# Input projections in groups of two or three column tiles, with 128 of the 576 tokens as the stationary operand

## The chip, the cores and the metric

The kernel runs on one core of one Trainium2 chip. The metric is device time in microseconds of one execution. The engines are named as the profile names them: PE is TensorE (PEld its weight loads), DVE is VectorE, ACT is ScalarE, POOL is GpSimd, SP is SyncE, which issues all DMAs here.

## The reference

One step of a hybrid encoder layer, for a prompt of 512 tokens and a sample of 64 tokens, 2048 channels:

```
mod = silu(c) @ w_ada + b_ada;  shift, scale, gate = split(mod)
h = rmsnorm(x) * (1 + scale) + shift
q|k|v|z_att|u_ssm|z_ssm|u_pool|z_pool = h @ w_in      # 2048 x 6144
y_att  = chunk-band attention (16 heads of 64, relative bias)
y_ssm  = complex-diagonal state-space scan of u_ssm -> gelu -> GLU
y_pool = trailing means (2/4/8/16) of u_pool minus token, linear, scale
y = concat(rmsnorm_b(y_b) * silu(z_b))
x = x + gate * (y @ w_out);  final rmsnorm
```

It returns the layer's output, the keys and values, and the states. All is float32. The kernel keeps float32 accuracy in its large products by splitting each operand into a rounded part and a rest (h into `hh` and `hl`, a weight into `wh` and `wl`) and adding three passes: hh by wh, hl by wh, hh by wl.

## The kernel before, in words

All 576 tokens (512 prompt, 64 sample) go together. Activations lie with channels on partitions and tokens along the free dimension, in tiles of four blocks of 128 channels (`ck`, 14 buffers). The 6144 columns of w_in are 48 column tiles of 128.

- First block (to about 139 us): adaLN, norm and modulation, one 128-channel block at a time, and with it six of the column tiles (`first_tiles`: Q, K of head pairs 0 and 1, V of pairs 0 and 2). Its order is written out by hand. Their results for the prompt lie in six PSUM banks, four of them of pool `pp` (`fA`, `fB`).
- Attention stage (139 to about 490 us): the other 22 tiles of V, K, Q and u, one column tile at a time by `proj_steps` (L486), interleaved with the attention of eight head pairs (`att_units`). `evac_q`, `evac_k` and `evac_v` empty a projection's PSUM.
- Gate and pool stage (490 to about 697 us): 16 tiles (z of attention, u and z of pooling) interleaved with the state-space branch (`s5_units`), evacuated by `gate_z` and `pool_branch`.
- GLU, then the last four z tiles (751 to 803 us), then the output product and final norm.

`proj_steps` computes one column tile in 16 steps, one for each block of 128 channels. A step issues six matmuls: three passes, each for two halves of 288 tokens, with the weight block stationary and the tokens moving. The result takes a tile of two PSUM banks from `pp`, which has two such tiles, so that one is filled while the other is emptied. The other four banks are pool `pm` (`mtile`), used by attention, the scan and all small products.

Weights come in chunks of 128x1024 (eight channel blocks of one column tile). `w_next` loads and splits ahead: a chunk is loaded by SP, cast by ACT into `wh` (L146), and DVE subtracts to get `wl` (L70, a helper for all subtractions), up to two chunks ahead of the one in use; each of the three kinds of buffer has three copies.

`evac_q` empties a Q tile for two heads: for each head, ACT writes the rounded part to one half of the partitions, then DVE writes the rest to the other half:

```
A.activation(Q1[a, c0:c0 + n], ps[a], AF.Copy, scale=0.125)
stt(Q1[o, c0:c0 + n], ps[a], 0.125, Q1[a, c0:c0 + n].bitcast(F32), ALU.mult, ALU.subtract)
```

`gate_z` applies Silu on ACT into a single buffer `z` and then multiplies on DVE.

`interleave(gens, units, total)` sets the order in which the code writes projection steps and units: one unit after so many steps. Outside the blocks with a hand-written order, a planner then sets the order on each engine: it simulates the program with its own durations and takes, of the instructions that are ready, the one written first. So an engine's order needn't be the code's. At run time each engine follows its fixed order and waits where it must. The planner also keeps two engines from one PSUM bank at a time, by waits.

Of the kernel before, what the change touches and what calls it, by code (L numbers as in the profile page):

```python
# [17 lines left out]
NP = 512  # L18
# [3 lines left out]
HC = NT // 2  # L22
NH = 16
# [8 lines left out]
S5_SPREAD = 231  # L32
# [16 lines left out]
def kernel(ctx, tc, xp, xs, xT, cT, wada_ss, wada_g, bsh, bsc, bgate, ng, wf1, wrest,  # L49
# [68 lines left out]
    pp = psctx.enter_context(tc.tile_pool(name="pp", bufs=2, space=PSUM))  # L118
# [4 lines left out]


    wsrc = [wrest[r, :, 8 * h:8 * h + 8] for r in range(38) for h in range(2)]
    wsrc += [wglu[f] for f in range(4)]
    wsrc += [wrest[r, :, 8 * h:8 * h + 8] for r in range(38, 42) for h in range(2)]
# [4 lines left out]
    def w_load():  # L132
        n = wstate[0]
        t = wp.tile([128, 1024], F32, tag="wr", name="w", bufs=WR)
        src = wsrc[n]
        SY.dma_start(t.rearrange("p (a b) -> p a b", a=src.shape[1]), src)
        wraw[n] = t
        wstate[0] += 1

    def w_split():  # L140
        n = wstate[1]
        while wstate[0] <= n:
            w_load()
        t = wraw.pop(n)
        wh = wp.tile([128, 1024], F32R, tag="wh", name="wh")
        A.copy(wh, t)  # L146
        wl = wp.tile([128, 1024], F32R, tag="wl", name="wl")
        sub(wl, t, wh.bitcast(F32))
        wsplit[n] = (wh, wl)
        wstate[1] += 1  # L150
# [215 lines left out]
    warm = pp.tile([128, 2, 512], F32, tag="pj", name="warm")  # L366
    for n in range(WARM):
        PE.matmul(warm[:, 0, 0:128], ident, xc[3][:, WLANE, 0:128], start=True, stop=True)
# [19 lines left out]
    rb = pp.tile([128, 2, 512], F32, tag="pj", name="rb")  # L388
    rstdx = s1.tile([128, NT], F32, tag="rstdx", name="rstdx", bufs=1)
    for t in range(5):  # L390
        V.tensor_scalar(dg[:, t], ident, r[:, t:t + 1], None, op0=ALU.mult)
        if t < 4:
            PE.matmul(rb[:, 0, 128 * t:128 * t + 128], ones, dg[:, t], start=True, stop=True)
        else:
            PE.matmul(rb[:, 1, 0:64], ones, dg[:, t, 64:128], start=True, stop=True)
    split_w(0)
    ada_sel(0)
    A.copy(rstdx[:, NP:NT], rb[:, 1, 0:64])
    A.copy(rstdx[:, 0:NP], rb[:, 0])

    fA = pp.tile([128, 2, 512], F32, tag="pj", name="fA")
    fB = pp.tile([128, 2, 512], F32, tag="pj", name="fB")
    fC = mtile("fC")
    fD = mtile("fD")
    fS = mtile("fS", (128, 384))
    f1p = [fA[:, 0], fA[:, 1], fB[:, 0], fB[:, 1], fC, fD]
# [79 lines left out]
    def f1_pieces(f):  # L486
        return [(f1p[f], 0, NP), (fT[:, 64 * f:64 * f + 64], NP, NS)]
# [3 lines left out]
    def proj_steps(done):  # L491

        ps = pp.tile([128, 2, 512], F32, tag="pj", name="pj")
        for k in range(KT):
            if k % 8 == 0:
                wh, wl = w_next(8)
            c, i = divmod(k, 4)
            for ws, hs, first, last in ((wh, hh, True, False), (wh, hl, False, False), (wl, hh, False, True)):
                for ch in range(2):
                    PE.matmul(ps[:, ch, 0:HC], ws[:, k % 8], hs[c][:, i, HC * ch:HC * ch + HC],  # L500
                              start=(k == 0 and first), stop=(k == KT - 1 and last))
            if k == KT - 1:
                nxt = done(ps)
                if callable(nxt):
                    pend.append(nxt)
            yield
            if k in (2, 7, 12) and pend:
                nxt = pend.pop(0)()
                if callable(nxt):
                    pend.append(nxt)  # L510

    def pj_pieces(ps):
        return [(ps[:, 0, 0:HC], 0, HC), (ps[:, 1, 0:NP - HC], HC, NP - HC), (ps[:, 1, NP - HC:HC], NP, NS)]

# [17 lines left out]
    kvs, Q1s, Tbs = {}, {}, {}  # L532
# [9 lines left out]
    def kv_load(j):  # L542
        kv = ck("kv", F32, (128, 2304))
        kf, vf = kv[:, 0:704], kv[:, 704:704 + NT]
        vt = kv[:, 1280:2048].rearrange("p (b d) -> p b d", b=6)
        SY.dma_start(kf[:, NP:NP + 128], ckT[j])
        SY.dma_start(vt[:, 4], cv[:, j])
        G.memset(vt[64:128, 5], 0.0)
        kvs[j] = (kf, vf, vt)

# [4 lines left out]
    def evac_q(j, pieces):  # L555
        Q1 = ap1.tile([128, 2 * NT], F32R, tag="Q1", name="Q1", bufs=2)
        Q1s[j] = Q1
        for ps, t0, n in pieces:
            for h in range(2):
                a, o = halves[h]  # L560
                c0 = q_col(h, t0)
                A.activation(Q1[a, c0:c0 + n], ps[a], AF.Copy, scale=0.125)
                stt(Q1[o, c0:c0 + n], ps[a], 0.125, Q1[a, c0:c0 + n].bitcast(F32), ALU.mult, ALU.subtract)

    def evac_k(j, pieces):
        kf = kvs[j][0]
        for ps, t0, n in pieces:
            o = t0 if t0 < NP else 640
            A.copy(kf[:, o:o + n], ps)
        SY.dma_start(k_o[j, :, 0:NP], kf[:, 0:NP])  # L570
        SY.dma_start(k_o[j, :, NP:NT], kf[:, 640:704])

    def evac_v(j, pieces):
        if j not in kvs:
            kv_load(j)
        vf = kvs[j][1]
        for ps, t0, n in pieces:
            V.tensor_copy(vf[:, t0:t0 + n], ps)

    def att_units(j):  # L580
# [15 lines left out]
        def vtr():  # L596
            pv = mtile("pv", (128, 4, 128))
            for i in range(4):
                PE.transpose(pv[:, i], vf[:, 128 * i:128 * i + 128], ident)
            pw = mtile("pw", (128, 128))  # L600
            PE.transpose(pw[0:64], vf[:, NP:NT], ident)
            A.copy(vt[:, 0:4], pv)
            A.copy(vt[0:64, 5], pw[0:64])
# [90 lines left out]
    kv_load(2)  # L694
    first.close()
    evac_v(0, f1_pieces(2))
    evac_k(0, f1_pieces(1))
    evac_q(0, f1_pieces(0))
    evac_q(1, f1_pieces(3))
    evac_k(1, f1_pieces(4))  # L700
    evac_v(2, f1_pieces(5))

    def proj_v(j):
        yield from proj_steps(lambda ps: evac_v(j, pj_pieces(ps)))

    def proj_kq(j):
        att_load(j)
        for e in (evac_k, evac_q):
            yield from proj_steps(lambda ps, e=e: e(j, pj_pieces(ps)))

    def proj_u(f):
        yield from proj_steps(lambda ps: evac_u(f, ps))
# [3 lines left out]
    def evac_u(f, ps):  # L716
        if f == 0:
            uTs.append(ck("uT"))
        A.copy(uTs[0][:, f].rearrange("p (c t) -> p c t", c=2), ps[:, :, 0:HC])

    interleave([proj_v(1), proj_kq(2), proj_v(3)], att_units(0) + att_units(1), 64)
    for j in range(2, 7):
        units = att_units(j)
        interleave([proj_kq(j + 1), proj_v(j + 2) if j < 6 else proj_u(0)], units, 48)
    interleave([proj_u(f) for f in range(1, 4)], att_units(7), 48)
# [6 lines left out]
    ysp0 = yp_.tile([128, 8, 128], F32R, name="ysp0")  # L732
# [163 lines left out]
    def gate_z(y, ps):  # L896
        z = zp.tile([128, 2, HC], F32, tag="z", name="z")
        with tc.high_priority():
            A.activation(z, ps[:, :, 0:HC], AF.Silu)
        yv = y.rearrange("p (c t) -> p c t", c=2)  # L900
        mul(yv, yv, z)
# [7 lines left out]
    def gate_att(f, ps):  # L909
        y = y_att[f // 4][:, f % 4]  # L910
        stt(y, y, prm[:, 3, f:f + 1], ssqa, ALU.mult, ALU.mult)
        gate_z(y, ps)
# [8 lines left out]
    ypool = []  # L921

    def pool_branch(g, ps):
        wn = 2 << g
# [7 lines left out]
        for pv_, t0, n in pj_pieces(ps):  # L932
            o = 15 + t0 if t0 < NP else 542
            A.copy(e[:, o:o + n], pv_)
# [43 lines left out]
    gens = [proj_steps(lambda ps, f=f: gate_att(f, ps)) for f in range(8)]  # L978
    gens += [proj_steps(lambda ps, g=g: pool_branch(g, ps)) for g in range(4)]
    gens += [proj_steps(lambda ps, f=f: gate_z(ypool[0][:, f], ps)) for f in range(4)]  # L980
# [22 lines left out]
    for f in range(4):  # L1003
        wh, wl = w_next(4)
        ps2 = {}
        for part in (1, 0):
            if part == 0:
                pg_ = pp.tile([128, 2, 512], F32, tag="pj", name="pg")
                ps = [pg_[:, chn, 0:HC] for chn in range(2)]
# [11 lines left out]
        stt(y_ssm[:, f].rearrange("p (c t) -> p c t", c=2), pg_[:, :, 0:HC], bg[:, f:f + 1], sg, ALU.add, ALU.mult)  # L1021
# [24 lines left out]
    interleave([proj_steps(lambda ps, f=f: gate_z(y_ssm[:, f], ps)) for f in range(4)], [ssm_scale], 4)  # L1046
# [8 lines left out]
    ysp1 = fin.tile([128, 8, 128], F32R, name="ysp1", bufs=1)  # L1055
    ysp = [(ysp0, ysp1)[k // 8][:, k % 8] for k in range(KT)]
# [208 lines left out]
def _layout(i):  # L1265
# [64 lines left out]
_INS = ["xp", "xs", "xT", "cT", "wada_ss", "wada_g", "bsh", "bsc", "bgate", "ng", "wf1", "wrest", "ext", "ckT", "cv",  # L1330
# [40 lines left out]
```

## Time and profile before

| | |
|---|---|
| median of 3 runs | 1023.0 us (1022.98 to 1025.25) |
| profiled execution | 1021.69 us, span 1019.9 us |
| PE busy | 995.2 us, 7032 matmuls |
| DVE busy | 708.4 us |
| ACT busy | 456.8 us |

The span runs from the first to the last instruction; the profiled execution's own time is 1.8 us longer. Busy time is a union of an engine's instructions. A matmul's duration is a latency that overlaps its neighbours, so what it costs is read from the distance between starts.

### The profile page before, as it was taken

To read this page: it belongs to the slowest core of one execution; us is meant where nothing else is said; L and a number is where in the kernel's file an instruction comes from. 1 tells how busy PE (TensorE), PEld (TensorE's weight loads), DVE (VectorE), ACT (ScalarE), POOL (GpSimd) and SP (SyncE) were. 2 spreads that over 40 slices of the span, in tenths; PEclk is the share of its full clock that TensorE was granted. 3 is DMA by queue.
4 is the path that set the end of the run, shared out by engine and by line. 5 is a ranking of instruction groups with operands and counts; after the bars stand their busy time and mean duration, and the time that the engine had idled before them with its cause. 6 is when DMAs were issued, how large, how long until landed. Compare 5 with 4: busy or idle time off the path is not lost.

```text
span 1019.9 us, 17854 instructions
## 1 busy us (share of the span) xinstructions
PE 995.2 (98%) x7032; PEld 904.5 (89%) x7032; DVE 708.4 (69%) x1654; ACT 456.8 (45%) x873; POOL 7.1 (1%) x52
## 2 busy tenths in 40 slices
PE   4999999999999999999999999999999999999996
PEld 3666689999999999999999999999999988888885
DVE  5677785745555564644699897995353699988876
ACT  5332365635354453543835554658452414131325
POOL 0000000000000000000000000000000000000000
PEclk9999999999999999999999999999999999999998
DMA  9999652332333333222222212222322685646425
GB/s 365 412 417 388 239 174 78 100 103 89 88 95 98 100 96 100 75 74 83 66 79 77 84 63 86 78 66 67 100 84 83 234 297 181 226 142 207 140 92 196
DMA packets 51572, 148.45 MB, mean 146 GB/s; under 512 B 9312, under 2 KB 18528, under 8 KB 46816
## 3 DMA queue, kind: packets, MB, share of 16 engines
q1 hardware_dynamic: 51488, 147.31, 42.7%
q8 instruction: 55, 0.90, 0.4%
q14 instruction: 29, 0.24, 0.1%
HBM read 137.75 MB, written 9.53 MB: 144 GB/s over the span
## 4 chain that ended last, share of the span: by engine, by line
PE 96%; DMA 1%; DVE 1%; ACT 1%; SPq 0%; issue 0%; DVEq 0%
PE pj L500 52%; PE po L1128 6%; PE po L1127 6%; PE po L1129 6%; PE pa L330 3%; PE sps L629 2%; PE tp L645 2%; PE av L656 2%; PE po L1132 1%; PE po L1131 1%; PE pg L1016 1%; PE pgb L1016 1%; PE fS L442 1%; PE fA L436 1%; DMA xc<-in_xT_dram 1%; PE yp L885 1%
## 5 line engine op out<-in xcount | busy, mean ns | idle before, releaser
L500 PE MATMUL pj<-hh,wh 128*128 128x288 f32 x1344 | 298.0, 303 | 0.0
L500 PE MATMUL pj<-hh,wl 128*128 128x288 f32 x1344 | 287.8, 296 | 0.0
L500 PE MATMUL pj<-hl,wh 128*128 128x288 f32 x1344 | 287.7, 296 | 0.0
L500 PEld LDWEIGHTS pj<-hh,wh 128*128 128x128 f32 x1344 | 214.8, 189 | 3.4 <-issue 0.8
L500 PEld LDWEIGHTS pj<-hh,wl 128*128 128x128 f32 x1344 | 216.2, 188 | 0.1
L500 PEld LDWEIGHTS pj<-hl,wh 128*128 128x128 f32 x1344 | 215.6, 188 | 0.1
L146 ACT CAST wh<-w 128x1024 fp32r<-128x1024 f32 x120 | 125.8, 1049 | 176.5 <-PE po L1131 97.6
L70 DVE TENSOR_TENSOR wl<-w,wh 128x1024 fp32r<-128x1024 f32 x120 | 146.6, 1222 | 82.3 <-ACT wh L146 81.2
L1128 PE MATMUL po<-wl,yh 128*128 128x512 f32 (+1 forms) x256 | 99.0, 387 | 0.0
L1127 PE MATMUL po<-wh,yh 128*128 128x512 f32 (+1 forms) x256 | 99.0, 387 | 0.0
L1129 PE MATMUL po<-wh,yl 128*128 128x512 f32 (+1 forms) x256 | 99.0, 387 | 0.0
L76 DVE SCALAR_TENSOR_TENSOR acc<-ada,scT,acc 128x512 f32<-128x512 f32 x120 | 83.0, 747 | 0.5
L631 DVE CUSTOM_DVE_ANT_0 P<-sps,Tb 128x128 f32<-128x128 f32 (+2 forms) x80 | 36.9, 462 | 47.5 <-PE sps L629 41.3
L634 ACT ACTIVATE P<-P,s 128x128 f32<-128x128 f32 (+4 forms) x72 | 39.7, 551 | 66.2 <-DVE s L633 65.8
L1127 PEld LDWEIGHTS po<-wh,yh 128*128 128x128 f32 x256 | 48.1, 188 | 9.9
L1128 PEld LDWEIGHTS po<-wl,yh 128*128 128x128 f32 x256 | 48.1, 188 | 9.8
L1129 PEld LDWEIGHTS po<-wh,yl 128*128 128x128 f32 x256 | 48.1, 188 | 9.8
L629 PE MATMUL sps<-K,Q 128*128 128x128 f32 (+4 forms) x160 | 35.0, 307 | 0.1
L635 DVE RECIPROCAL s<-s 128x1 f32<-128x1 f32 x72 | 11.7, 163 | 33.4 <-ACT P L634 32.9
L650 ACT COPY PT<-tp 128x256 f32<-128x256 f32 (+1 forms) x40 | 18.3, 458 | 31.7 <-PE tp L645 31.5
L645 PE MATMUL tp<-ident,P 128*128 128x128 f32 x176 | 31.1, 273 | 0.0
L67 DVE TENSOR_TENSOR ssqa<-ssqa,sq 128x576 f32<-128x576 f32 x7 | 5.3, 761 | 37.1 <-ACT sq L672 37.1
(330 smaller groups left out, 1381.7 us busy)
## 6 DMA issues: line engine op xcount, KB each, us to landing
w<-in_wrest_dram SPq DMA_DIRECT2D x84, 512.0 KB, 3.7
ada<-in_wada_ss_dram SPq DMA_DIRECT2D x22, 1024.0 KB, 9.0
w<-in_wout_dram SPq DMA_DIRECT2D x32, 512.0 KB, 3.7
ada<-in_wada_g_dram SPq DMA_DIRECT2D x32, 512.0 KB, 4.5
adac<-in_wada_ss_dram SPq DMA_DIRECT2D x10, 1024.0 KB, 14.0
w<-in_wf_dram SPq DMA_DIRECT2D x16, 384.0 KB, 11.2
xc<-in_xT_dram SPq DMA_DIRECT2D x8, 576.0 KB, 7.4
Tb<-in_ext_dram SPq DMA_DIRECT2D x8, 512.0 KB, 3.7
```

The costliest lines, as they stand in the source:

```text
L70: V.tensor_tensor(o, a, b, op=ALU.subtract)
L76: V.scalar_tensor_tensor(o, in0=a, scalar=s, in1=b, op0=op0, op1=op1)
L146: A.copy(wh, t)
L330: PE.matmul(pa[32 * g:32 * g + 32, 0:256], sc[:, k], adat[b, k // 8][:, k % 8], start=(k < 4), stop=(k >= KT - 4))
L500: PE.matmul(ps[:, ch, 0:HC], ws[:, k % 8], hs[c][:, i, HC * ch:HC * ch + HC], start=(k == 0 and first), stop=(k == KT - 1 and last))
L629: PE.matmul(ps[:, n], qs, K[z][:, g, k0:k0 + nk], start=(z == 0), stop=(z == 1))
L631: V.tensor_tensor_reduce(out=p[r, 0:nk], in0=ps[r, n], in1=Tb[r, g, ::-1][:, b0:b0 + nk], scale=1.0, scalar=-3.0e38, op0=ALU.add, op1=ALU. ...
L634: A.activation(p[:, 0:nk], p[:, 0:nk], AF.Exp, bias=s4[:, 1:2], accum_out=s4[:, 2:3])
L645: PE.transpose(tp[:, kb], p[:, 128 * kb:128 * kb + 128], ident)
L1127: PE.matmul(po[t], yh[c][:, ci, s_], wh[:, i], start=f0, stop=False)
L1128: PE.matmul(po[t], yh[c][:, ci, s_], wl[:, i], start=False, stop=False)
L1129: PE.matmul(po[t], yl[c][:, ci, s_], wh[:, i], start=False, stop=l0)
```

## The change

Projections are computed in groups. Ten groups have three column tiles (K, Q, V of a head pair for pairs 2 to 7; two tiles of z_att with one of u_pool, four times), six have two (u_ssm, z_pool, z_ssm). For the first 448 tokens (NA) the weights stay stationary and one matmul of 448 columns takes the place of a half. For the last 128 tokens (NB: 64 of the prompt and the sample's 64) the tokens are stationary and the group's weights move, 384 or 256 columns at once. That result has tokens on partitions; it is copied to SBUF and transposed back by PE, tile by tile (`bt`), except V, which attention wants that way.

Pool `pp` becomes four tiles of one bank. A group of three takes all four. Weight chunks hold two channel blocks of three tiles (128x768) or four of two tiles (128x1024). In the last chunk of a group the 128 tokens come first, then the tiles one after another. The first block computes K, V, Q of pairs 0 and 1. The interleaving counts are adapted (ATT_SPREAD, S5_SPREAD), the sample's split buffers `ysp0` and `ysp1` hold 4 and 12 tiles instead of 8 and 8, and the GLU takes two one-bank tiles.

```diff
+NA = 448
+NB = NT - NA
-    pp = psctx.enter_context(tc.tile_pool(name="pp", bufs=2, space=PSUM))
+    pp = psctx.enter_context(tc.tile_pool(name="pp", bufs=4, space=PSUM))
...
-    def proj_steps(done):
-        ps = pp.tile([128, 2, 512], F32, tag="pj", name="pj")
-        for k in range(KT):
-            if k % 8 == 0:
-                wh, wl = w_next(8)
-            c, i = divmod(k, 4)
-            for ws, hs, first, last in ((wh, hh, True, False), (wh, hl, False, False), (wl, hh, False, True)):
-                for ch in range(2):
-                    PE.matmul(ps[:, ch, 0:HC], ws[:, k % 8], hs[c][:, i, HC * ch:HC * ch + HC],
-                              start=(k == 0 and first), stop=(k == KT - 1 and last))
...
+    def proj_group(done, done_b, bs):
+        nf = len(done)
+        kc = 2 if nf == 3 else 4
+        n = 0
+        for ch in range(KT // kc):
+            last = ch == KT // kc - 1
+            wh, wl = w_next(kc)
+            if ch == 0:
+                pa = [pjtile("pj") for _ in range(nf)]
+                pb = pjtile("pjb")
+            parts = list(range(nf)) + [nf]
+            if last:
+                parts = parts[-1:] + parts[:-1]
+            for f in parts:
+                for kk in range(kc):
+                    k = kc * ch + kk
+                    c, i = divmod(k, 4)
+                    f0, l0 = k == 0, k == KT - 1
+                    if f < nf:
+                        wsl = slice(128 * f, 128 * f + 128)
+                        PE.matmul(pa[f][:, 0:NA], wh[:, kk, wsl], hh[c][:, i, 0:NA], start=f0, stop=False)
+                        PE.matmul(pa[f][:, 0:NA], wh[:, kk, wsl], hl[c][:, i, 0:NA], start=False, stop=False)
+                        PE.matmul(pa[f][:, 0:NA], wl[:, kk, wsl], hh[c][:, i, 0:NA], start=False, stop=l0)
+                    else:
+                        o = pb[:, 0:128 * nf]
+                        PE.matmul(o, hh[c][:, i, NA:NT], wh[:, kk], start=f0, stop=False)
+                        PE.matmul(o, hh[c][:, i, NA:NT], wl[:, kk], start=False, stop=False)
+                        PE.matmul(o, hl[c][:, i, NA:NT], wh[:, kk], start=False, stop=l0)
+                    if l0 and f == nf:
+                        b_ = bs()
+                        nt = b_.shape[1] // 128
+                        with tc.high_priority():
+                            A.copy(b_, pb[:, 0:128 * nt])
+                    if l0 and f < nf:
+                        nxt = done[f](pa[f][:, 0:NA])
+                        if callable(nxt):
+                            pend.append(nxt)
+                    if l0 and f == nf - 2:
+                        bt = mtile("bt", (128, nt, 128))
+                        for g in range(nt):
+                            PE.transpose(bt[:, g], b_[:, 128 * g:128 * g + 128], ident)
+                        done_b(bt, pb)
+                    yield
...
+    def group_kqv(j):
+        def b(bt, pb):
+            vt = kvs[j][2]
+            V.tensor_copy(vt[64:128, 3], pb[0:64, 256:384])
+            V.tensor_copy(vt[0:64, 5], pb[64:128, 256:384])
+            evac_k(j, [(bt[:, 0], NA, NB)])
+            store_k(j)
+            evac_q(j, [(bt[:, 1], NA, NB)])
+        return proj_group([lambda ps, e=e: e(j, [(ps, 0, NA)]) for e in (evac_k, evac_q, evac_v)], b,
+                          lambda: (kv_load(j), kvt[j][:, 2048:2304])[1])
...
+    def z_a(y, ps):
+        z = zp.tile([128, NA], F32, tag="z", name="z")
+        with tc.high_priority():
+            A.activation(z, ps, AF.Silu)
+        mul(y[:, 0:NA], y[:, 0:NA], z)
```

## Rows read from the trace of the kernel before

**Rows 1.** The page, busy us of each engine, share of the span, instructions.
```profile
PE 995.2 (98%) x7032; PEld 904.5 (89%) x7032; DVE 708.4 (69%) x1654; ACT 456.8 (45%) x873; POOL 7.1 (1%) x52
```

**Rows 2.** The page, chain that ended last: shares of the span.
```profile
PE 96%; DMA 1%; DVE 1%; ACT 1%; SPq 0%; issue 0%; DVEq 0%
```

**Rows 3.** Waits: who waited for whom: us in total, times, longest.
```profile
PE warm L368 <- DMA xc<-in_xT_dram: 14.0, 1, 14.0
...
ACT Q L562 <- DVE Q L76: 9.6, 13, 0.9
```

**Rows 4.** The page, costliest groups: busy us, mean ns, idle before.
```profile
L500 PE MATMUL pj<-hh,wh 128*128 128x288 f32 x1344 | 298.0, 303 | 0.0
```

**Rows 5.** The chain in order of time: start us, us, what.
```profile
507.54 0.87 PE xtp L791 x8
...
699.07 26.38 PE pj L500 x198
...
755.76 47.60 PE pj L500 x357
```

**Rows 6.** Timeline of PE, output stage: start us, us, engine, line, operation.
```profile
809.80 0.39 PE L1128 MATMUL po<-wl,yh 128*128 128x512 f32 x1
...
815.92 0.39 PE L1127 MATMUL po<-wh,yh 128*128 128x512 f32 x1
...
1006.32 0.28 PE L1127 MATMUL po<-wh,yh 128*128 128x256 f32 x1
...
1008.00 0.28 PE L1129 MATMUL po<-wh,yl 128*128 128x256 f32 x1
```

**Rows 7.** Windows: length, busy of PE, PEld, DVE, ACT, POOL, clock, DMA, GB/s.
```profile
139.00:490.00 351.00, 350.85 (x2689) 337.29 (x2689) 199.26 (x554) 169.45 (x367) 4.62 (x37) 1.00 0.30 94
490.00:697.00 207.00, 207.00 (x1596) 204.20 (x1595) 183.10 (x434) 116.90 (x229) 0.33 (x3) 1.00 0.26 78
```

**Rows 8.** Timeline of ACT and DVE in the attention stage, Q's evacuation.
```profile
237.89 0.78 ACT L592 CAST K<-kv 64x704 fp32r<-64x704 f32 x1
...
239.42 0.39 ACT L562 ACTIVATE Q<-pj 64x288 fp32r<-64x288 f32 x1
...
240.31 0.45 DVE L76 SCALAR_TENSOR_TENSOR Q<-pj,Q 64x288 fp32r<-64x288 f32 x1
...
242.45 0.46 DVE L76 SCALAR_TENSOR_TENSOR Q<-pj,Q 64x288 fp32r<-64x288 f32 x1
...
247.88 0.23 DVE L76 SCALAR_TENSOR_TENSOR Q<-pj,Q 64x64 fp32r<-64x64 f32 x1
```

**Rows 9.** Timeline, end of the first block: Q of pair 0 evacuated.
```profile
135.50 0.59 ACT L562 ACTIVATE Q<-fA 64x512 fp32r<-64x512 f32 x1
...
137.56 0.69 DVE L76 SCALAR_TENSOR_TENSOR Q<-fA,Q 64x512 fp32r<-64x512 f32 x1
```

**Rows 10.** Timeline of ACT and DVE, gate and pool stage, Silu and product.
```profile
517.11 0.64 ACT L899 ACTIVATE z<-pj 128x576 f32<-128x576 f32 x1
...
525.66 0.75 DVE L64 TENSOR_TENSOR yatt<-yatt,z 128x576 f32<-128x576 f32 x1
...
567.00 1.28 ACT L899 ACT_TABLE_LOAD   x1
568.30 0.65 ACT L899 ACTIVATE z<-pj 128x576 f32<-128x576 f32 x1
...
570.96 0.75 DVE L64 TENSOR_TENSOR yatt<-yatt,z 128x576 f32<-128x576 f32 x1
```

**Rows 11.** Groups by line: weight splits of 1024 and 768 columns, ACT, DVE.
```profile
L146 ACT CAST wh<-w 128x1024 fp32r<-128x1024 f32 x120 | 125.8, 1049 | 176.5 <-PE po L1131 97.6 <-PE pj L500 54.9 <-PE pg L1016 8.5
...
L382 ACT CAST w1h<-w 128x768 fp32r<-128x768 f32 x16 | 13.1, 821 | 4.2 <-DMA w<-in_wf_dram 4.2
...
L70 DVE TENSOR_TENSOR wl<-w,wh 128x1024 fp32r<-128x1024 f32 x120 | 146.6, 1222 | 82.3 <-ACT wh L146 81.2 <-DMA ER<-in_scr_dram 0.6
...
L70 DVE TENSOR_TENSOR w1l<-w,w1h 128x768 fp32r<-128x768 f32 x16 | 15.3, 954 | 4.1 <-ACT w1h L382 4.1
```

More of the change, by code (lines that the diff above doesn't have):

```diff
@@ L122, in mtile, with pjtile, group_chunks @@
         return pm.tile(list(shape), F32, tag="m", name=name)
-    wsrc = [wrest[r, :, 8 * h:8 * h + 8] for r in range(38) for h in range(2)]
+    def pjtile(name, shape=(128, 512)):
+        return pp.tile(list(shape), F32, tag="pj", name=name)
+    def group_chunks(groups, g3, g2):
+        out = []
+        for g in groups:
+            if len(g) == 3:
+                out += [wg3[g3, :, 2 * n:2 * n + 2] for n in range(8)]
+                g3 += 1
+            else:
+                out += [wg2[g2, :, 4 * n:4 * n + 4] for n in range(4)]
+                g2 += 1
+        return out
+    wsrc = group_chunks(GROUPS, 0, 0)
     wsrc += [wglu[f] for f in range(4)]
-    wsrc += [wrest[r, :, 8 * h:8 * h + 8] for r in range(38, 42) for h in range(2)]
+    wsrc += group_chunks(GROUPS_Z, 10, 4)
     wsrc += [wout[n, kk] for n in range(4) for kk in range(8)]
@@ L364 @@
     V.tensor_scalar(prm[:, 1], prm[:, 1], 1.0, None, op0=ALU.add)
-    warm = pp.tile([128, 2, 512], F32, tag="pj", name="warm")
+    warm = pjtile("warm")
     for n in range(WARM):
-        PE.matmul(warm[:, 0, 0:128], ident, xc[3][:, WLANE, 0:128], start=True, stop=True)
+        PE.matmul(warm[:, 0:128], ident, xc[3][:, WLANE, 0:128], start=True, stop=True)
     pss = mtile("pss", (128, 8))
@@ L387 @@
     dg = wp.tile([128, 5, 128], F32, tag="wh", name="dg")
[L388 removed]
+    rb = [pjtile("rb") for _ in range(2)]
     rstdx = s1.tile([128, NT], F32, tag="rstdx", name="rstdx", bufs=1)
@@ L392 @@
         if t < 4:
-            PE.matmul(rb[:, 0, 128 * t:128 * t + 128], ones, dg[:, t], start=True, stop=True)
+            PE.matmul(rb[0][:, 128 * t:128 * t + 128], ones, dg[:, t], start=True, stop=True)
         else:
-            PE.matmul(rb[:, 1, 0:64], ones, dg[:, t, 64:128], start=True, stop=True)
+            PE.matmul(rb[1][:, 0:64], ones, dg[:, t, 64:128], start=True, stop=True)
     split_w(0)
     ada_sel(0)
[L398 to L404, printed above, removed]
+    A.copy(rstdx[:, NP:NT], rb[1][:, 0:64])
+    A.copy(rstdx[:, 0:NP], rb[0])
+    f1p = [pjtile("f1") for _ in range(4)] + [mtile("f1m") for _ in range(2)]
     fS = mtile("fS", (128, 384))
-    f1p = [fA[:, 0], fA[:, 1], fB[:, 0], fB[:, 1], fC, fD]
     blk = {}
@@ L714 @@
-    uTs = []
[L716 to L725, printed above, removed]
+    for z in range(2):
+        evac_k(0, f1_piece(0, z))
+        evac_v(0, f1_piece(1, z))
+        evac_q(0, f1_piece(2, z))
+        evac_k(1, f1_piece(3, z))
+        evac_v(1, f1_piece(5, z))
+        evac_q(1, f1_piece(4, z))
```

195 lines of the change are left out of this document (119 added, 76 removed).

## The prediction

> **What bounds the kernel now.** I read the page's busy times first: PE is busy 995.2 of 1019.9 us, DVE 708.4, ACT 456.8 [rows 1]. A busy PE alone says little, so next the chain that ended last: 96% of it is PE [rows 2]. Then the waits: the one long wait of PE is the 14.0 us for the first inputs [rows 3]. So from 14 us to the last matmuls PE issues back to back, and the time is the sum of what PE issues. The largest item, among the costliest groups, is the projection matmul of line 500, three groups of 1344 with 288 columns each [rows 4]. Last I read what one matmul costs. The mean duration there (303 ns) is a latency that overlaps the next; the cost is the spacing of starts. In the chain, 198 such matmuls take 26.38 us and 357 take 47.60 us, 133.3 ns each [rows 5]. In the timeline, 27 steps of 512 columns take 6.12 us, 226.7 ns each, and 14 steps of 256 columns take 1.68 us, 120.0 ns each [rows 6]. The three lie on one line: 106.7 ns for 256 more columns, 0.4167 ns a column, which leaves 13.3 ns that every matmul pays whatever its width. The granted clock is 1.00 in the two stages that hold 38 of the 42 tiles that change [rows 7], the 2.4 GHz level, so no part of the change can win clock there.
>
> **The matmuls.** Before: 42 column tiles x 16 row blocks x 3 passes x 2 halves = 4032 of 288 columns, 4032 x 133.3 = 537.6 us. After: a group of 3 issues, per row block, 9 of 448 columns and 3 of 384; a group of 2 issues 6 of 448 and 3 of 256. With 10 groups of 3 and 6 of 2 that is 2016 of 448, 480 of 384 and 288 of 256, 2784 in all. The columns are the same number (1,161,216). From the line, 448 costs 200.0 ns, 384 costs 173.3, 256 costs 120.0: 403.2 + 83.2 + 34.6 = 521.0 us. It saves 16.6 us, which is 1248 x 13.3 ns. By part: 9.0 us in the attention stage (22 tiles), 6.4 in the gate and pool stage (16), 1.3 in the last four tiles. Widths 448 and 384 lie between measured ones; tokens as stationary operand are the form that the output stage already runs (512 columns of weights moving) [rows 6]. So I bound the saving from 15.6 to 17.6 us.
>
> The Trainium skill, TensorE: Matmul & The Clock Gate, section Back-to-back issue gap, gives a warm gap of N/2.4 + 2.5 ns. By that rule 1248 fewer matmuls save only 3.1 us. The trace disagrees with it at three widths, 13.3 ns instead of 2.5.
>
> **The transposes.** The 128 tokens' result comes out with tokens on partitions and is transposed back. Six attention groups add 2 each, the two u groups 2, four z/pool groups 3, four z groups 2: 36. For pairs 2 to 7 the V transposes fall from 5 to 4, 6 fewer. Net 30. Eight of the same shape and type take 0.87 us in the chain, 109 ns each [rows 5]: +3.3 us, all on PE. Net of both: -13.3 us, 1021.69 - 13.3 = 1008.4 for the profiled run if PE still never waits.
>
> **Work off PE.** Weight chunks become 128x768 in the groups of 3: 8 per group where three tiles had 6, so 104 chunks in place of 84, of which 80 take DVE 954 ns and ACT 821 instead of 1222 and 1049 [rows 11]; +3 us on each engine over the whole kernel. Evacuations are the same columns in more pieces, split 448 + 128. All of it lies beside PE: DVE is busy 199 of 351 us in the attention stage and 183 of 207 in the gate and pool stage [rows 7]. The second is near its limit: after, I estimate 185 of 202 us. Loads land as before, a chunk is loaded and split two chunks ahead, 9.3 us (48 matmuls) instead of 12.8 (96); cast plus subtraction of one take under 2.3 us. Stores of K move behind the transposed part on SP, past no load that has less than that lead. I cost these at nothing; the bounds are 0 and 3 us. The first block computes the same six tiles in another column order (Q, K, V of pairs 0 and 1); 0, within 1 us either way. The out stage gets more of its sample split after the pools close, needed 12 us after its start (two steps of 28 matmuls of 227 ns): 0.
>
> **The handover of the PSUM banks**, the one real unknown. Before, a tile has two banks and a second pair is free while it is emptied: 12.8 us of cover. After, a group of 3 takes all four banks of its pool. In its last chunk it finishes the 128 tokens first, then its three tiles, 1.2 us each (6 matmuls of 200 ns). The next group wants the first bank at once, so each bank must be empty 2.4 us after its last matmul. If it isn't, the matmul that waits holds everything behind it on PE's queue, attention and transposes too, and the other engines have no more slack than PE then.
> - Bank of K: one ACT copy, 0.6 us. Bank of V: one DVE copy, 0.7 us. Covered.
> - Bank of Q: four operations that alternate ACT, DVE, ACT, DVE, each waiting for the one before (ACT waits for DVE's Q 13 times [rows 3]). At the end of the first block, for 512 columns and little beside them, they took 135.50 to 138.25 = 2.75 us [rows 9]. In the attention stage four operations of 288 columns took 239.42 to 242.91 = 3.5 us, and the whole of a tile 8.7 us [rows 8].
> - Banks of the z tiles: Silu into one buffer z, which the next Silu can use only after DVE's product has read it. A table load adds 1.28 us; DVE's product began 2.0 us after Silu's end in one case (568.95 to 570.96) and 7.9 us after it in another [rows 10]. Two tiles now want z 1.2 us apart.
>
> For 448 columns I take the Q chain at 4 us, between those rows. Against 2.4 us that is 1.6 us late. What can fill it: attention matmuls of the unit that falls there (0.3 to 0.5 us), and the next group's work for the other banks, which depends on nothing that is late (1.2 us for the third tile, 1.0 for the tokens). The order on the engines is not the code's: K's split of pair 3 is written after Q's evacuation of that pair, and ran ahead of it [rows 8]. So the planner can fill, as far as its durations are right. From below: 0. From above, the 8.7 us chain with nothing filled: 6.3 us at each of 6 attention groups, 38 us, and some 1 us at each of the ten other groups, 48 us. I take 0.25 us a boundary, 16 boundaries, 4 us: near the lower end, because the row with the right number of operations is 3.5 us and 2.2 us of other PE work is at hand. Sum: 1008.4 + 4 = 1012.4 for a run like the profiled one. The median before (1023.0) is 1.3 us above that run; single runs differ by as much, and I predict 1012.5 as the median.
>
> The Trainium skill, Perfetto Trace Analysis, section Matmuls, asks that independent matmul groups rotate through different PSUM banks, so that the evacuation of one overlaps the next group's matmuls. This change does the opposite in the groups of 3. No run here shows yet what that costs; by it the fourth case below is what happens.
>
> **Rivals.**
> 1. PE never waits (0 to 1 us): 1008.4 to 1009.4. For it: 98% busy PE, a planner that moves work. Against it: a static order with 2.4 us of cover where the rows show chains of 3.5 us.
> 2. DVE becomes the bound of the gate and pool stage: it is busy 88% there already, and late products hold z and with it banks. Then that stage keeps its 207 us and the 4.6 us won there (6.4 less 16 transposes) are gone: about 1017.
> 3. The 13.3 ns doesn't go with the count of matmuls but with their columns (133.3 / 288 = 0.463 ns a column). Then the same columns cost the same, nothing is saved, and the 3.3 us of transposes stay: 1025.0, just slower. Against it: 512 columns would then take 237 ns, where the rows have 226.7, and 256 would take 118.5, where they have 120.0 [rows 6]. The skill's gap of 2.5 ns, named above, would put the same case at 1021.9.
> 4. Slower: the handover of Q's bank. If PE keeps the code's order and the contended chain is between 4.2 and 8.7 us, say 6.4, it is 4.0 us late at 6 boundaries, 24 us, and 0.6 us at ten others, 6 us: 1008.4 + 30 = about 1038. It decides the sign from 13.3 us of stalls, 0.8 us a boundary, and is slower beyond doubt from 1.0 us (16.4 us). For it: the rows of Q and z above. Against it: PE has 2.2 us of other work at each boundary, and DVE is busy only 57% in the attention stage.
>
> **Chances.** Forecast (stalls of 1 to 7 us, 1009.4 to 1015.4): 0.50. Rival 1: 0.15. Rival 2: 0.08. Rival 3: 0.04, at the edge of 0.3%, half to either side. Rival 4: 0.23, of which 0.08 ends within 0.3%. A measurement of this kernel tells 0.3%, 3.1 us, from no change: faster 0.50 + 0.15 + 0.08 = 0.73; same 0.02 + 0.08 = 0.10; slower 0.02 + 0.15 = 0.17. Range: from 1007 (rival 1 less the 1 us by which the saving may be larger, and the runs' spread) to 1024, where rival 4's lower part ends; what is left out is the 0.15 or so above and some 0.03 below.
>
> **What would show it.** Starts of the 448-column matmuls 200 ns apart, of 384 173 ns, of 256 120 ns; if they are 220 apart or more, the saving is wrong. 36 new transposes at 109 ns. Busy PE about 982 us. At group boundaries, idle time of PE before the first matmul into a new group's second tile, ended by ACT or DVE Q, or by z: 4 us in all by my sum, 16 or more if rival 4 holds. The order of the new group's parts in the timeline says whether the planner filled. If DVE is over 95% busy from 490 to 690 us and PE waits on its products, rival 2. My forecast is wrong if stalls come to under 1 or over 7 us, or if a stall lies elsewhere, as at a weight chunk.

## The result, and the profile after

The changed kernel takes 1031.0 us (median of 4 runs, 1027.8 to 1031.5), the kernel before 1023.0 (4 runs, 1022.8 to 1025.3): ratio 1.0067, interval [1.0054, 1.0079]. It is slower by 8 us, where 10.5 us less were forecast. The profiled execution took 1031.48 us, with a span of 1029.7.

Busy time on the page of the changed kernel, against [rows 1]:
```profile
PE 997.7 (97%) x5814; PEld 868.2 (84%) x5814; DVE 710.2 (69%) x1674; ACT 462.2 (45%) x900; POOL 7.3 (1%) x52
```
1218 fewer instructions on PE, 2.5 us more busy time. 982 us were forecast.

PE's waits (against [rows 3]):
```profile
PE warm L390 <- DMA xc<-in_xT_dram: 13.9, 1, 13.9
PE bt L558 <- ACT bS L550: 5.1, 3, 3.7
...
PE pg L1228 <- DVE al L77: 0.8, 1, 0.8
```
The new wait is that of the transposes for ScalarE's copy of the 128-token result. The two windows of [rows 7], and three short ones inside the second:
```profile
139.00:490.00 351.00, 351.00 (x2040) 318.35 (x2040) 201.43 (x556) 172.49 (x374) 4.98 (x38) 1.00 0.32 94
490.00:697.00 207.00, 202.97 (x1135) 187.07 (x1134) 176.02 (x431) 114.72 (x230) 0.34 (x3) 0.98 0.27 77
529.00:533.00 4.00, 0.99 (x5) 0.57 (x4) 2.89 (x8) 2.08 (x9) 0.00 (x0) 0.94 0.28 89
533.00:539.00 6.00, 5.31 (x16) 4.79 (x17) 2.12 (x4) 5.84 (x17) 0.00 (x0) 0.50 0.00 0
539.00:545.00 6.00, 6.00 (x34) 5.70 (x33) 6.00 (x17) 2.53 (x7) 0.00 (x0) 0.97 0.50 134
```
The attention stage has no stall. In the gate and pool stage PE stands still for most of 529 to 533 us, and for the 6 us behind that the clock is granted at 0.50 (1.2 GHz); then it is back. The timeline of PE at that place, and then that of ScalarE (start us, us, operation, in brackets the idle time before it and what ended it):
```profile
526.23 0.33 PE L545 MATMUL pjb<-wh,hl 128*128 128x384 f32 x1
...
529.62 0.37 PE L540 MATMUL pj<-hh,wl 128*128 128x448 f32 x1
533.69 0.90 PE L558 MATMUL bt<-ident,bS 128*128 128x128 f32 x3 [3.69 <-ACT bS L550]
534.24 0.72 PE L538 MATMUL pj<-hh,wh 128*128 128x448 f32 x1
```
```profile
525.20 0.23 ACT L915 COPY Kc<-km 128x96 f32<-128x96 f32 x1
530.83 2.44 ACT L919 COPY Mo<-Kc 32x128 f32<-32x128 f32 x9 [5.40 <-DVE Kc L83]
533.17 0.46 ACT L550 COPY bS<-pjb 128x384 f32<-128x384 f32 x1
```
The copy bS could have begun at 526.6, when the last matmul of the 128 tokens (pjb) ended, 3.2 us before the transposes' turn. It stood in ScalarE's queue behind the copies that build Mo (a matrix of the state-space branch, made from Kc), and their first waited 5.40 us for VectorE's Kc. The kernel before has the same queue, here in ScalarE's timeline:
```profile
526.88 1.05 ACT L146 CAST wh<-w 128x1024 fp32r<-128x1024 f32 x1
530.60 4.27 ACT L835 COPY Mo<-Kc 32x128 f32<-32x128 f32 x16 [2.67 <-DVE Kc L76]
534.89 1.05 ACT L146 CAST wh<-w 128x1024 fp32r<-128x1024 f32 x1
535.84 0.64 ACT L899 ACTIVATE z<-pj 128x576 f32<-128x576 f32 x1
```
There ScalarE was kept from the tile's evacuation until 535.84 and PE waited for nothing, since the next tile had its own pair of banks: the evacuated tile's last matmul began at 530.61, and the first one that needed its banks again began at 544.51.

Where the time is, stage by stage, from the starts of PE's matmuls in the traces (us; each of the first three stages runs up to the next one's first projection matmul, "start" from the first matmul of all; "last four" ends at the last projection matmul, and "output" is the rest up to the last matmul; e-numbers are the runs below):

| | start | attention | gate and pool | last four | output |
|---|---|---|---|---|---|
| before | 124.80 | 350.03 | 262.06 | 52.17 | 207.46 |
| before, again (e8) | 126.17 | 350.04 | 262.06 | 52.16 | 207.48 |
| e5, before with Mo on GpSimd | 127.75 | 350.00 | 262.27 | 52.17 | 207.45 |
| changed | 127.75 | 347.78 | 269.73 | 51.72 | 208.64 |
| e1, no wait at the transposes | 126.18 | 347.78 | 269.33 | 51.66 | 210.85 |
| e2, Mo on GpSimd | 126.17 | 347.78 | 263.41 | 51.67 | 207.97 |
| e3, transposes last | 126.14 | 348.12 | 267.56 | 51.56 | 208.85 |
| e7, 300 steps | 126.20 | 347.78 | 276.39 | 51.66 | 208.28 |
| e9, Mo on GpSimd, 300 steps | 126.26 | 347.78 | 269.64 | 51.66 | 208.93 |
| e10, Mo on GpSimd, 340 steps | 127.76 | 347.78 | 264.05 | 51.69 | 207.96 |
| e11, Mo on GpSimd, transposes last | 127.78 | 347.78 | 262.83 | 51.53 | 208.82 |

The attention stage won 2.2 us (9.0 less 1.1 for ten more transposes was forecast), the gate and pool stage lost 7.7. The start's 2.9 are not the change's: the kernel before shows starts of 124.80, 126.17 (e8) and 127.75 us (e5, the same code up to there).

The saving itself is small because a 448-column matmul isn't 200 ns. The timeline of PE in the changed kernel, starts only at the ends of two runs of such matmuls:
```profile
674.91 0.36 PE L538 MATMUL pj<-hh,wh 128*128 128x448 f32 x1
...
678.97 0.36 PE L540 MATMUL pj<-hh,wl 128*128 128x448 f32 x1
...
681.37 0.37 PE L538 MATMUL pj<-hh,wh 128*128 128x448 f32 x1
...
684.26 0.36 PE L540 MATMUL pj<-hh,wl 128*128 128x448 f32 x1
```
20 steps in 4.06 us are 203.0 ns; 14 in 2.89 are 206.4. Two paces, and neither is 200. (In the three short windows above, the eighth column is the granted clock, as in [rows 7].)

### The profile page after: what moved, and what is told of

Same layout as the page of the kernel before. It is cut to its first block, busy times and chain, and to the rows that moved or that the text cites. A ratio compares the mean times of both kernels' runs of the same rounds, so it can differ in the third digit from the quotient of the medians.

```text
span 1029.7 us, 15564 instructions
## 1 busy us (share of the span) xinstructions
PE 997.7 (97%) x5814; PEld 868.2 (84%) x5814; DVE 710.2 (69%) x1674; ACT 462.2 (45%) x900; POOL 7.3 (1%) x52
## 5 line engine op out<-in xcount | busy, mean ns | idle before, releaser
L538 PE MATMUL pj<-hh,wh 128*128 128x448 f32 x672 | 256.8, 382 | 0.0
L540 PE MATMUL pj<-hh,wl 128*128 128x448 f32 x672 | 246.9, 367 | 0.0
L539 PE MATMUL pj<-hl,wh 128*128 128x448 f32 x672 | 246.7, 367 | 0.0
L168 ACT CAST wh<-w 128x768 fp32r<-128x768 f32 (+1 forms) x140 | 129.6, 926 | 214.6 <-PE po L1251 85.5
L77 DVE TENSOR_TENSOR wl<-w,wh 128x768 fp32r<-128x768 f32 (+1 forms) x140 | 149.6, 1068 | 94.8 <-ACT wh L168 94.2
L540 PEld LDWEIGHTS pj<-hh,wl 128*128 128x128 f32 x672 | 126.7, 189 | 10.9
L538 PEld LDWEIGHTS pj<-hh,wh 128*128 128x128 f32 x672 | 127.0, 189 | 10.2 <-issue 0.2
L539 PEld LDWEIGHTS pj<-hl,wh 128*128 128x128 f32 x672 | 127.2, 189 | 8.2
L543 PE MATMUL pjb<-wh,hh 128*128 128x384 f32 (+1 forms) x256 | 83.7, 327 | 0.0
L544 PE MATMUL pjb<-wl,hh 128*128 128x384 f32 (+1 forms) x256 | 81.0, 316 | 0.0
```

The lines of the kernel that those rows point to most:

```text
L77: V.tensor_tensor(o, a, b, op=ALU.subtract)
L538: PE.matmul(pa[f][:, 0:NA], wh[:, kk, wsl], hh[c][:, i, 0:NA], start=f0, stop=False)
L539: PE.matmul(pa[f][:, 0:NA], wh[:, kk, wsl], hl[c][:, i, 0:NA], start=False, stop=False)
L540: PE.matmul(pa[f][:, 0:NA], wl[:, kk, wsl], hh[c][:, i, 0:NA], start=False, stop=l0)
L543: PE.matmul(o, hh[c][:, i, NA:NT], wh[:, kk], start=f0, stop=False)
L544: PE.matmul(o, hh[c][:, i, NA:NT], wl[:, kk], start=False, stop=False)
```

## Experiments

**e1, no wait at the transposes.**
```
-PE.transpose(bt[:, g], b_[:, 128 * g:128 * g + 128], ident)
+PE.transpose(bt[:, g], hh[g][:, 0, 0:128].bitcast(F32), ident)
```


> The transposes of the 128-token results read columns of hh, which is complete since the first stage, instead of ScalarE's copy bS; the copy still runs, and K, Q, u, z and e of tokens 448 to 575 are wrong. So PE can't wait there for ScalarE; all else is as in the changed kernel. Theory 1 (the three waits of the transposes for the copy, 5.6 us in the trace, and the half clock behind the longest, 2.6 us, are what turned a small gain into a loss): the 4.06, 1.49 and 0.67 us gaps are gone, the window 490 to 540 shows granted clock 1.00, and the time falls by 7 to 9 us, to 1022 to 1024. Theory 2 (VectorE, late by that much in the gate and pool stage, is what bounds it): the wait comes back within some 20 us at another operation that needs VectorE (gp, yp or the next weight split), and the time stays above 1028. Theory 3 (the loss is in the spacing of the 448-column matmuls and in the first 27 us, and gaps of this size are made up by a later one): under 3 us less, 1028 to 1031.


Measured: 1030.8 us. Theory 1 falls as I put it. The wait came back at once, at two other operations, as PE's waits in e1 show (gp is a product of the state-space branch):
```profile
PE gp L931 <- DVE tA L71: 2.4, 1, 2.4
PE pj L538 <- ACT bS L550: 2.2, 1, 2.2
PE po L1248 <- DVE wl L77: 1.7, 1, 1.7
```
The second is the next group's first matmul, which needs a bank that ScalarE has not emptied: the same copy bS, still behind Mo. So the transposes are only the first to need ScalarE there. What theory 2 asked for came as well: a wait for VectorE at gp, 4.3 us later, and a time above 1028. The clock was granted at 0.50 again behind the two waits (538 to 540 us).

**e2, Mo on GpSimd.**
```
-A.copy(Mo[32 * s:32 * s + 32, f, s:4], Kc[32 * f:32 * f + 32, 0:4 - s])
+G.tensor_copy(Mo[32 * s:32 * s + 32, f, s:4], Kc[32 * f:32 * f + 32, 0:4 - s])
```


> Only the 64 small copies that build Mo go from ScalarE to GpSimd, which has little to do. In the trace of the changed kernel nine of a set of sixteen (2.44 us, behind 5.4 us of waiting for Kc) stood on ScalarE ahead of the copy bS that the transposes at 533 us wait for. Theory 1: that gap (4.06 us) and the half clock behind it (2.6 us) go, the other two gaps (1.49 and 0.67) stay: 6 to 7 us less, 1024 to 1025. Theory 2 (VectorE is late, and ScalarE's queue stops for something of VectorE anyway): the copy bS then stands behind the next operation of ScalarE that needs VectorE, a gap of 1 to 4 us stays in that place, and the time is above 1028. Third: the copies take longer on GpSimd than on ScalarE and the product with Mo (yp) waits for them: PE waits at yp, 1030 or more.


Measured: 1022.6 us (10 runs), 8.4 less than the changed kernel; against the kernel before 0.9994 [0.9985, 1.0004]. Of the difference between the two profiled executions 6.3 us are in the gate and pool stage; 1.6 are the start, which is chance. ScalarE's timeline in e2:
```profile
525.58 0.48 ACT L550 COPY bS<-pjb 128x384 f32<-128x384 f32 x1 [0.16 <-PE pjb L545]
526.08 1.28 ACT L983 ACT_TABLE_LOAD   x1
527.37 0.54 ACT L983 ACTIVATE z<-pj 128x448 f32<-128x448 f32 x1
532.59 0.54 ACT L983 ACTIVATE z<-pj 128x448 f32<-128x448 f32 x1 [4.67 <-DVE yatt L71]
```
bS now follows its matmul by 0.16 us. GpSimd's timeline has the sixteen copies that took ScalarE 4.27 us in the kernel before, and no other engine waits for them:
```profile
529.87 7.81 POOL L919 COPY Mo<-Kc 32x128 f32<-32x128 f32 x16 [56.76 <-DVE Kc L83]
```
Of PE's waits in that stage, 0.8 us at gp for VectorE and 0.5 at the transposes are left.

**e3, transposes last.** The block of transposes moves ahead of the call of `done[f]`, and:
```
-if l0 and f == nf - 2:
+if l0 and f == nf - 1:
```

> The transposes stand behind the last column tile of their group instead of the last but one: one tile's six or twelve matmuls (1.2 or 2.4 us) more between the 128-token product and the transposes that need ScalarE's copy of it. Theory 1: gaps under 1.2 us go, the one of 4.06 us shrinks to 1.5 to 2.9 and the half clock with it may stay or go; the time falls by 3.5 to 8 us, to 1023 to 1027.5. Rival (what comes out of the transposes is now late: evacuation of K and Q in the attention stage, e of the pool branch, and the 128-token bank is held longer): a wait at the next group's first use of a bank or at sps, and the time is 1030 or more.


Measured: 1027.5 us, 1.0043 [1.0029, 1.0057]. In the range, at its end: two gaps went, 0.7 us at gp and 0.3 at tp came, the long one shrank to the row here (PE's waits in e3; 1.5 to 2.9 was expected), and the window 490 to 540 still has a clock of 0.97.
```profile
PE bt L554 <- ACT bS L550: 3.0, 1, 3.0
```

**e5, the kernel before with Mo on GpSimd** (e2's edit).

> The kernel before, with its 64 Mo copies on GpSimd as in e2; nothing of the change. It says whether the 8.4 us of e2 belong to the change or would have been there without it. Theory 1 (ScalarE stopped behind Mo's wait for VectorE in the kernel before too, but no bank or transpose needed ScalarE in that stretch): no difference, 1022 to 1024. Theory 2 (the copies delay the kernel before as well): 3 to 8 us less, 1015 to 1020. Third (GpSimd's copies hinder VectorE): 1026 or more.


Measured: 1023.4 us (11 runs), 1.0005 [0.9996, 1.0014]. Theory 1: what e2 gave back was the change's own loss, not a weakness that the kernel before shares.

**e7, one number.**
```
-S5_SPREAD = 320
+S5_SPREAD = 300
```


> The changed kernel with one number altered: the SSM's units are spread over 300 steps of the projections instead of 320, so that Kc and the Mo copies fall at other places between the ends of the groups. Theory 1 (a set of Mo copies that waits for VectorE stands ahead of the evacuations at the end of a group, and that is a matter of how the two lie to each other): the waits of PE in the gate and pool stage change place and size, and the time differs from 1031 by more than 2 us in either direction, between 1023 and 1036. Rival (VectorE and ScalarE are short of time in this stage however the units lie): 1029 to 1033.


Measured: 1036.1 us, at the upper end of theory 1 and outside the rival's bounds: how the SSM's units lie to the ends of the groups is worth 5 us. PE's largest waits in e7:
```profile
PE bt L558 <- ACT bS L550: 6.0, 2, 5.3
PE pj L538 <- ACT wh L168: 2.4, 1, 2.4
```
The first is the changed kernel's place: in e7 all sixteen copies of Mo, and a cast of weights, stand ahead of bS. The second is new, at 718 us: a weight chunk that ScalarE has cast too late, the place that the prediction named as a sign of being wrong.

**e9, e7 with e2's edit.**

> The 300 steps of e7 together with the Mo copies on GpSimd of e2. Theory 1 (ScalarE's queue, stopped by Mo's wait for VectorE, is what the spread shifted in e7): with the copies away from ScalarE the spread hardly matters, 1021 to 1025, and PE waits under 2 us in the gate and pool stage. Rival (VectorE itself is late there, and the copies are only one of several carriers of that): part of e7's 13 us stays, 1027 to 1034, with PE waiting for ScalarE or VectorE in the same places.


Measured: 1029.6 us. Both are half right. The copies carry 6.5 us again (8.4 in e2), but 6.9 us against e2 stay, with VectorE first among PE's waits in e9:
```profile
PE gp L931 <- DVE tA L71: 3.5, 1, 3.5
PE pj L538 <- ACT wh L168: 2.4, 1, 2.4
```
The late weight chunk of e7 is still there, at 711 us, so it isn't Mo's. In the 6 us ahead of it ScalarE is busy for 5.91, and from 694 to 709 us it loads a table six times (1.28 us each), changing between gT, z and ssqp. So Mo's place in ScalarE's queue is the largest carrier of the loss and not the only one.

**e10, e2 with 340 steps** (`S5_SPREAD = 340`).

> e2 with the SSM's units spread over 340 steps instead of 320. Theory 1 as for the kernel with 300: 1021 to 1025; if the later units also end the 0.8 us wait at gp and the 0.5 us at the transposes, 1021 to 1022, a little under the kernel before. Rival (VectorE late): 1026 or more, or a wait at the end of the stage, where the gated SSM result is needed, of 1 us and more.


Measured: 1024.7 us, 1.0008 [0.9999, 1.0017]. The time is in theory 1's range, but 2.1 us above e2's: one wait of 2.4 us at po for VectorE, of the rival's kind, took the place of the ones at gp and the transposes. With the copies on ScalarE only 320 and 300 steps were run, so whether another spread alone would have avoided the stall is open.

**e11, e2 with the transposes last** in the gate and pool stage and the last four tiles only: e3's move, where the group is given `late_b=True`.

> e2, and in the groups of the gate and pool stage and the last four tiles the transposes stand behind the last column tile instead of the last but one. The stage takes 263.4 us in e2 and 262.1 in the kernel before; 1.3 us of e2's are waits of PE at gp and at the transposes. Theory 1: the waits at the transposes (0.5 us) go and nothing comes in their place: 1021.5 to 1022.5. Rival (the pool branch gets its last 128 tokens later, and VectorE's queue with it): waits of 1 us and more at po or gp, 1023.5 or more.


Measured: 1022.8 us (11 runs), 1.0002 [0.9993, 1.0011]. Between theory 1 and the rival: the waits at the transposes are gone, gp still waits 0.8 us for VectorE, and the stage is 0.6 us shorter than in e2, with a start 1.6 us longer in the profiled execution. No version here beats the kernel before by what can be measured.

**e6, the attention stage alone.** The groups of that stage's 22 tiles stay; from there on the code is that of before (`S5_SPREAD` 231 again), with a bank pool of its own:
```
 uT = uTs[0]
 at.close()
+ppx.close()
+pp = psctx.enter_context(tc.tile_pool(name="pq", bufs=2, space=PSUM))
```

> The change in the attention stage alone (22 of its 42 column tiles: six groups of three, two of two); the gate and pool stage, the SSM's gates and the GLU are those of the kernel before. In the traces the attention stage takes 350.0 us before and 347.8 after, in the changed kernel and in e1 and e2 alike. Theory 1 (the stages' costs add up, and all the loss is in the gate and pool stage and at the start): 2.2 us less than before, 1020 to 1022, or 1022 to 1023 if the first 27 us lose 1.4 us as in e1 to e3. Theory 2 (the saving of the groups is paid back later, because the gate and pool stage is bound by VectorE and ScalarE and not by PE): 1022.5 to 1024.5. Forecast of the prediction for this part (704 matmuls fewer at 13.3 ns, 20 transposes more at 109 ns): 7 us less, 1016.


Measured: 1023.9 us (11 runs), 1.0012 [1.0003, 1.0021]; theory 2's range, though not its mechanism. (The expectation miscounts the prediction's part: it is 672 matmuls fewer and ten transposes more, 7.9 us.) PE's projections take the same 286.65 us in the stage as in the changed kernel, but up to the next stage's first projection it ran 1.5 us longer, 1.1 of them four small matmuls (bps) that came ahead of that projection, and three new waits of PE sum to 2.1 us:
```profile
PE xtp L903 <- DVE X L74: 0.9, 1, 0.9
PE po L1239 <- ACT z L1011: 0.8, 1, 0.8
PE pj L576 <- ACT uT L819: 0.4, 1, 0.4
```
The last is at the first matmul into the bank pool that this version closes and opens again between the stages, which I had not priced. The 2.2 us of the stage recur in every run with the groups (1.9 in e3), and are small enough that three such waits eat them.

**e8, the kernel before again.**

> The kernel before once more, unaltered, for a second profile of its first 27 us: the granted clock there was 1.00 in its first profile, 0.88 in the changed kernel's and 0.94 in e1, e2 and e3, all with the same work in that stretch. Theory 1 (how long the half clock lasts there is a matter of the single execution): mean clock below 1.00 in 0 to 27 us, and PE's first projection group starts later than the 138.8 us after the span's start that the first profile showed. Rival (the change does it): 1.00 again and the same start within 0.3 us.


Measured: theory 1. The window of the first 27 us in e8, and then in the changed kernel (the eighth column is the clock):
```profile
0.00:27.00 27.00, 12.42 (x88) 10.61 (x88) 14.16 (x33) 14.04 (x24) 1.17 (x7) 0.94 0.94 367
```
```profile
0.00:27.00 27.00, 12.38 (x83) 10.12 (x84) 13.76 (x30) 13.34 (x22) 1.17 (x7) 0.88 0.94 367
```
The clock is 1.00, 0.94 or 0.88 in three executions of before's start (its first profile, e8, e5), and the start takes 124.8, 126.2 or 127.8 us. The prediction's sum was made on the one with the shortest start.

**e4, the pace of a 448-column matmul.** In each of six groups another form, chosen by the group's number (from 0), with the order of the tiles (1) or of the passes (5) changed in two:
```
+c0, nw = {2: (64, NA), 3: (0, 512), 4: (0, 480)}.get(form, (0, NA))
...
-PE.matmul(pa[f][:, 0:NA], wh[:, kk, wsl], hh[c][:, i, 0:NA], start=f0, stop=False)
...
+hhs, hls = hh[c][:, i, c0:c0 + nw], hl[c][:, i, c0:c0 + nw]
...
+PE.matmul(pa[f][:, 0:nw], wh[:, kk, wsl], hhs, start=f0, stop=False)
```

> Only for the spacing of the matmuls with 448 columns, 204.1 ns in the mean instead of the 200.0 forecast. The six groups of the attention stage each take another form (what they compute is partly wrong): group 1 as it is; 2: tile by tile inside each pass, so that one matmul after another writes another PSUM bank; 3: hh and hl columns 64 to 511 instead of 0 to 447; 4: 512 columns; 5: 480 columns; 6: the passes in the order hh by wh, hh by wl, hl by wh. Theory A (three matmuls in a row into one bank cost the extra 4 ns): group 2 shows 200 ns, the others but the widths 204. Theory B (the address of the columns): group 3 differs from 204 by more than 2 ns, group 2 does not. Theory C (the width itself: what is added to columns at 2.4 GHz is 13.3 ns only at some widths): groups 2, 3 and 6 stay within 202 to 207, 512 columns stand at 226.7 as in the output stage, and 480 columns at 213.3 or above it by 2 to 7 ns. The time of the whole says nothing here; the wider groups alone add some 5 us.


Measured, mean step in ns from one such matmul to the next in each group (steps over 260 left out): 205.1 as it is, 206.3 with a new bank each time, 204.1 with other columns, 230.2 at 512, 216.6 at 480, 203.7 with the passes in another order. In the changed kernel the same six groups have 205.1, 205.3, 204.1, 204.0, 204.2 and 203.4. Theories A and B fall. C is right in its core and wrong on 512. PE's timeline in e4, the ends of a run of 14 at 512 columns and one of 17 at 480:
```profile
307.50 0.39 PE L555 MATMUL pj<-hl,wh 128*128 128x512 f32 x1
...
310.45 0.39 PE L556 MATMUL pj<-hh,wl 128*128 128x512 f32 x1
...
364.27 0.38 PE L555 MATMUL pj<-hl,wh 128*128 128x480 f32 x1
...
367.74 0.38 PE L556 MATMUL pj<-hh,wl 128*128 128x480 f32 x1
```
13 steps in 2.95 us are 226.9 ns, the output stage's pace [rows 6]; 16 in 3.47 are 216.9. Most other runs of 512 begin with steps of 224 to 236 ns; they come down to 227 after four to seven of them, or end before. So 512 has a settled pace of 13.3 ns over its columns, which short runs don't reach, and 480 and 448 settle higher: 16.9 over, and 16 or 20.

**e12, the block with the weights moving made narrower**, by group (from 0):
```
+wb = {1: 256, 2: 128, 3: 0, 4: 256}.get(gno[0], 128 * nf)
...
-o = pb[:, 0:128 * nf]
-PE.matmul(o, hh[c][:, i, NA:NT], wh[:, kk], start=f0, stop=False)
...
+n_ = 128 * nf if f0 or l0 else wb
+o = pb[:, 0:n_]
+if n_:
+    PE.matmul(o, hh[c][:, i, NA:NT], wh[:, kk, 0:n_], start=f0, stop=False)
...
```

> The changed kernel, but in the attention stage the block with the weights moving has fewer columns at all k but the first and the last: group 1 of the six is as it was (384 columns), groups 2 and 5 have 256, group 3 has 128, group 4 leaves the block out, group 6 is as it was; K, Q and V of tokens 448 to 575 of groups 2 to 5 are partly wrong. In the trace of the changed kernel a 448-column matmul takes 205 to 206 ns in a run of them behind a 384-column block or the scores, and 202 to 203 ns behind transposes. Theory 1 (what stands ahead of a run of 448-column matmuls sets its pace): group 4 falls to 202 to 203 ns behind all but the scores, and groups 2 and 5 do so behind the narrower block, as the last four tiles, whose blocks have 256 columns, have 202.6. Rival (the attention stage's other work, or the place of the operands, sets it): all six groups stay at 203.5 to 205.5. The whole is some 30 us shorter for what is left out, which says nothing.


Measured as in e4: 205.1, 204.7, 206.0, 203.8, 203.7, 203.6 ns for groups 1 to 6. The rival, but for group 3, which is half a nanosecond above it: the narrower block does not bring 202.6, and leaving it out (group 4) gives 203.8. The means hide something, though. The runs directly behind a narrower block do fall, from 206.7, 206.7 and 206.6 ns in groups 2, 3 and 5 of the changed kernel to 204.3, 204.8 and 203.3, while runs behind transposes in groups 3 to 5 rise by 0.6 to 1.0 ns. So what stands ahead of a run has some part in its pace, as theory 1 had it, on 21 to 25 steps each, and isn't all of it. What picks the pace stays open. In the changed kernel, runs behind transposes take 202 to 203 ns and runs behind 384-column blocks or scores about 206; that is a pattern in the traces, not a cause shown.

## Why the prediction was wrong

- **The matmuls: this step failed.** Forecast: 1248 matmuls fewer, 13.3 ns each, 16.6 us. Measured where stalls are nearly gone (e2): PE's projection time (the sum of all steps from a projection matmul to the next matmul) falls from 548.55 to 544.34 us, 4.2. The 12.4 us that are missing, from the steps in the traces: 6.7 because undisturbed 448-column matmuls step 204.1 ns; 2.0 because the 288-column ones stepped 132.8, not 133.3; 1.7 at 384 columns (175.5 instead of 173.3) and at changes of width; 1.2 because the first matmul behind each block of new transposes takes 86 ns more; 0.8 of waits left. I drew a line through three widths, read two numbers off it between the points, and called that a bound of 1 us. Rival 3 gave the other end, no saving at all (its 0.463 ns a column puts 448 at 207.4 and 384 at 177.8; the steps are 204.1 and 175.5), and I gave it 0.04; the truth lay between the two. The Trainium skill's rule (TensorE: Matmul & The Clock Gate, Back-to-back issue gap), N/2.4 + 2.5 ns, which the page gives for a single isolated matmul, makes it, as an estimate, 3.1 us saved. That came closer to the 4.2 than my line did, with a gap that no width here shows.
- **The transposes: right.** The 36 transposes take 3.0 us and V's fall by 0.7: 2.3 net, 3.3 forecast. (The 1.2 us that the matmuls right behind them lose are counted above.)
- **The handover: the place was wrong, and the size came out near by chance.** 4 us were put on 16 boundaries, and argued from Q's bank at the six in the attention stage; there PE waited for nothing, in all six groups. 5.6 us (from start to start; 5.1 in the list of waits) came in the gate and pool stage, at transposes that I had priced but never asked for whom they wait, and 2.6 us of half clock followed (2.2 in projections, 0.4 in gp), which had no term: from a clock of 1.00 before [rows 7] I had only concluded that none can be won. The Trainium skill's page named in the prediction (Perfetto Trace Analysis, Matmuls) asks for banks that rotate. In e1 a bank is the second thing that PE waits for (2.2 us), which bears it out; the first was the transposes' input.
- **Off-PE work at nothing: wrong in kind.** In e2 the sum of ScalarE's and VectorE's work did fit. What did not fit is its order: ScalarE waits up to 5.4 us at one operation, with the evacuation behind it. The 12.8 us of cover that a tile's second pair of banks gave had hidden that; some 3 us don't (before, changed, e2, e5). In e7 and e9 ScalarE has a stretch that is simply full.
- **Rival 2** had the right stage. No version with the groups got it under the 262.06 us of before: the best is 262.83. But VectorE is not the bound in the sense of being full, at 176 of 207 us busy; it is late at single points (e9: 3.5 us at gp).
- **Rival 4** was right in sign and in kind (an evacuation that comes late at the end of a group), wrong in place and nearly four times too large (30 us; 8.2 with the half clock).

Of the 9.8 us between the two profiled executions the stages give: start +2.9 (chance), attention -2.2, gate and pool +7.7, last four -0.4, output +1.2; the rest lies behind PE's last matmul.

## What to carry to other kernels

When a change shortens the time between a result and its next use, list what stands ahead of the evacuation in its engine's queue and what each of those waits for: here a queue with one late operand cost nothing at 12.8 us of cover and some 6 us at 3. Before counting on a cost per matmul, find a row with the very width; between measured widths the pace was 2 to 4 ns a matmul off the line in the mean, and with the 0.5 ns by which the old width was cheaper that took some 10 of the 16.6 us. And take a second profile of the kernel before if the sum rests on one: its start alone moved by 3 us.

## What the runs showed that was not expected

- The step from one matmul to the next, less 0.4167 ns a column (the slope between 256 and 512 columns, [rows 6]): 12.8 ns at 288, 13.3 at 256 and 512 once settled, 16.9 at 480, 16 or 20 at 448. Order, bank and column offset changed the last by at most 1 ns (e4).
- A stall can cost clock behind it, and its length alone doesn't say whether. Behind 3.7 us in the changed kernel the clock was 0.50 for 6 us, 2.6 us lost; behind 3.0 us in e3 (534 to 537), behind 2.2 and 2.4 us in e1 (538 to 540) and behind 2.4 us in e7 and e9 (718 to 721, 712 to 715) it was 0.50 for a shorter time. Behind 3.5 us at gp in e9 (window 490 to 550) and 2.4 us at po in e10 (675 to 690) it stayed at 1.00.
- Moving 64 copies of 32 partitions from ScalarE to GpSimd raised the time of sixteen from 4.27 to 7.81 us, and the changed kernel was 8 us faster for it.
